# A two-layer attention / mLSTM step on one core: projection ahead of compression, page numbers read in eights, every order table written anew

## The chip, the cores and the metric

The kernel runs on one core of one Trainium2 chip. That core has a matrix engine (PE, with its weight loads shown apart as PEld), a vector engine (DVE), an activation engine (ACT), a general engine (POOL) and a sync engine (SP), whose queue issues most of the DMAs; ACT issues the rest. The metric is the device time of one execution in microseconds (us). Three runs of the kernel before took 1090.14, 1091.55 and 1093.12 us; their median is 1091.55 us.

## What is computed

One inference step of two layers, for a prompt of 512 tokens and 8 sample sequences with one new token each (520 token columns in all, width 1024). Layer 0 is sparse attention with three branches, layer 1 an mLSTM; a final norm follows. Cut to what this case touches:

```python
def nsa_project(h, w_in):                   # h = rmsnorm(x); one input projection
    p = h @ w_in                            # q | 6 k/v blocks of 256 columns | gates | z
    ...
def compress_branch(rows, pe, w1, b1, w2):  # rows: past pages and new tokens, two of the k/v blocks
    part = jnp.einsum('bnrchd,cjrde->bnjche', seg, w1r)     # segments of 16 rows, blocks of 32
    hid = ... + part[:, j:j + n_cmp, j]
    summ = jnp.einsum('bnche,ced->bnchd', jax.nn.silu(hid), w2)
def nsa_sample(h, cache_kv_l, cache_win_l, page_table, ...):
    past = cache_kv_l[page_table]           # 8 sequences x 8 pages of 128 rows
    ...                                     # attention over compressed, selected and window rows
# layer 1: mLSTM cell with its convolution, gates and matrix states; then rmsnorm
```

The results are the two outputs y, the new cache rows and the new states.

## The kernel before, in words

**Tiling.** Tokens lie along the free axis, 520 columns as two halves of 260 (`c` = 0 and 1); features lie on the 128 partitions. A product of float32 accuracy is three matmuls (`mm3`): weights and activations are each split into a high part (a rounded copy, `whi`, `hhi`, `phi`, `w1h`, made by ACT or by a copy on DVE, which the profile calls CAST) and a low part (the rest, `wlo`, `hlo`, `plo`, `w1l`, made by a subtraction on DVE or POOL); high times high, high times low and low times high are added in PSUM. `load_w` (L554) does this for one weight tile: a DMA to `wraw` (two buffers), `whi`, `wlo`.

**Stages.** There are seven lists of work, run one after the other: (1) norm of x, the 12 k/v projection tiles and the 16 compression units, with the gates (to about 224 us of the span, where PE ends its last transposes before the q projection); (2) the q and z projections (to about 330 us); (3) the attention units (to about 508 us); (4) the output projection and the mLSTM's input projection (to 673 us); (5) its z projection and gates (to 786 us); (6) the mLSTM cell (to about 1042 us); (7) the last of the output projection and the final norm.

**What sets the order.** In lists 1, 2, 4 and 7 every operation is recorded as a numbered piece, and a table of numbers (`CALLS0` to `CALLS3`) gives the order in which the pieces are issued. In lists 3, 5 and 6 operations carry names of what they read and write (class `Plan`), and the tables `ORDER0` to `ORDER2` give the order. Each engine then takes its own instructions strictly in that order, and waits with semaphores for the others. Tables `MOVED0` to `MOVED3` and `MOVEDP0` to `MOVEDP2` name pieces whose engine is exchanged (`swapped`): a high part from ACT to DVE or back, a subtraction, product or sum from DVE to POOL or back. Everything is issued through the recording layer, so nearly every instruction has line 498 in the profile, and tiles are told apart by name.

**List 1 in detail.** x comes in as `x_t`, four DMAs of half a column half each, into two of the three `praw` buffers; the first weight tile comes in two halves (`raw0`). `split_x` makes `hhi` and `hlo` of x; squares (`sq`) summed through a matmul with ones give the norm factor `rr`, which multiplies the projection only when PSUM is evacuated (`kvt<-mm,rr`). `kv_tile` (L843) is one projection tile: for each of the two column halves 24 matmuls (8 slices of three passes) in a PSUM bank of the kind `mm`, of which there are two. `cmp_unit` (L763) is one compression unit: eight pages of 128 KB from the cache (`pages`, L755) into one `praw` buffer, their high and low parts, and 48 matmuls against `w1`. A page's DMA takes its address from the page table in SBUF: SP reads one number into a register, checks it, and issues the DMA. `KB` is a tile of 128x4096 that POOL fills with zeros; `hlo_113` and `hhi_107` of the rows below are column half 0, `hlo_137` and `hhi_119` half 1 (in the changed program 192, 179 and 240, 219).

Of the kernel before, what the change touches and what calls it, by code (L numbers as in the profile page):

```python
# [17 lines left out]
T, NB, NTOK = 512, 8, 520  # L18
# [96 lines left out]
)  # L115
ORDER1 = (
# [418 lines left out]
def step_kernel(ctx, tc, ap):  # L535
# [22 lines left out]
    def mmb():  # L558
        return bank("mm", 2)
# [2251 lines left out]
```

## Time and profile before

| | |
|---|---|
| median of three runs | 1091.55 us |
| the profiled execution | 1091.77 us, of it 1089.9 us span |
| mean granted PE clock | 0.986 |
| PE busy | 1044.1 us (96%), 8567 instructions |
| DVE, ACT, POOL busy | 792.9, 578.4, 276.6 us |
| DMA | 197.18 MB, mean 181 GB/s |

Busy time by list, from the windows of the same execution:

| list | us of the span | PE | DVE | ACT | POOL | DMA share |
|---|---|---|---|---|---|---|
| 1 | 0 to 224 | 203.43 | 140.97 | 86.89 | 58.22 | 0.46 |
| 2 | 224 to 330 | 103.67 | 65.49 | 43.20 | 34.78 | 0.35 |
| 3 | 330 to 508 | 173.05 | 156.13 | 128.54 | 14.38 | 0.46 |
| 4 | 508 to 673 | 164.04 | 124.99 | 76.52 | 54.61 | 0.48 |
| 5 | 673 to 786 | 111.57 | 73.83 | 74.87 | 28.25 | 0.74 |
| 6 | 786 to 1042 | 252.98 | 198.14 | 152.73 | 75.47 | 0.80 |
| 7 | 1042 to 1090 | 35.34 | 33.40 | 15.62 | 10.93 | 0.34 |

"Busy" counts an engine as busy while any of its instructions is under way. Matmuls overlap, so a busy PE can still run below its pace; the count of matmuls in a stretch of fixed length tells that, and PEclk the clock that was granted. The chain of waits is followed back from the last instruction: at each step to what released it. A DMA queue of SP is shown as SPq; its instructions are not counted as busy time.

### The profile page before, as it was taken

How to read it: one execution, taken by the hardware profiler on the slowest of the kernel's cores; microseconds unless marked ns; L12 is line 12 of the kernel's file. 1: busy time of each engine (PE TensorE's matmuls, PEld its weight loads, DVE VectorE, ACT ScalarE, POOL GpSimd, SP SyncE). 2: the span in 40 equal slices, each digit the busy share in tenths (PEclk: the TensorE clock that was granted, in tenths of full speed). 3: DMA queues.
4: the chain of work that ended last, by engine and by line, in shares of the span. 5: the costliest groups of instructions: out<-in, count | busy, mean ns of one | idle time of the engine just before them, and what ended most of it. 6: DMA issues, size and time to landing. Idle time of an engine off the chain costs nothing.

```text
span 1089.9 us, 23970 instructions
## 1 busy us (share of the span) xinstructions
PE 1044.1 (96%) x8567; PEld 927.1 (85%) x8567; DVE 792.9 (73%) x1981; ACT 578.4 (53%) x1324; POOL 276.6 (25%) x301
## 2 busy tenths in 40 slices
PE   5999999999999999999999999999999999999996
PEld 4999899989998787778999999799867588887885
DVE  6856663578539899885788786757576778677886
ACT  5233243433358687773444455667666665654533
POOL 2215142222240100101234322231221333222322
PEclk9999999999999999999999999999999999999998
DMA  6454543233334642365543552878787789888542
GB/s 212 149 171 154 163 149 112 83 111 100 125 93 126 186 118 69 118 206 200 177 139 106 172 181 61 290 246 303 253 302 281 246 289 318 281 285 276 173 132 83
DMA packets 124793, 197.18 MB, mean 181 GB/s; under 512 B 16117, under 2 KB 66166, under 8 KB 124418
## 3 DMA queue, kind: packets, MB, share of 16 engines
q1 hardware_dynamic: 118194, 185.58, 52.4%
q10 hardware_dynamic: 6480, 10.08, 2.6%
q8 instruction: 67, 1.10, 0.4%
q14 instruction: 52, 0.43, 0.1%
HBM read 145.89 MB, written 58.10 MB: 187 GB/s over the span
## 4 chain that ended last, share of the span: by engine, by line
PE 75%; DVE 11%; ACT 5%; issue 3%; DMA 3%; SPq 2%; POOL 0%; POOLq 0%; DVEq 0%; ACTq 0%
PE mm L498 48%; PE s L498 15%; PE t L498 7%; PE d L498 5%; ACT s L498 2%; DVE s L498 2%; SPq L498 2%; DVE wlo L498 1%; DVE x L498 1%; DMA praw<-in_cache 1%; DMA wraw<-in_m_out 1%; DVE qst L498 1%; DVE sm L498 1%; ACT pt L498 1%; DMA wraw<-in_w_kv 1%
## 5 line engine op out<-in xcount | busy, mean ns | idle before, releaser
L498 PE MATMUL mm<-hhi,whi 128*128 128x260 f32 x976 | 282.4, 289 | 4.6 <-DVE kvt L498 3.2
L498 PE MATMUL mm<-hlo,whi 128*128 128x260 f32 x976 | 277.9, 285 | 4.1 <-DVE hlo L498 4.1
L498 PE MATMUL mm<-hhi,wlo 128*128 128x260 f32 x976 | 278.5, 285 | 2.0 <-DVE wlo L498 1.6
L498 PEld LDWEIGHTS mm<-hhi,whi 128*128 128x128 f32 x976 | 184.9, 189 | 10.1 <-DVE kvt L498 3.7
L498 PEld LDWEIGHTS mm<-hlo,whi 128*128 128x128 f32 x976 | 184.6, 189 | 5.0 <-DVE hlo L498 4.5
L498 PEld LDWEIGHTS mm<-hhi,wlo 128*128 128x128 f32 x976 | 184.8, 189 | 2.9 <-DVE wlo L498 2.3
L498 POOL TENSOR_TENSOR wlo<-wraw,whi 128x1024 fp32r<-128x1024 f32 (+1 forms) x50 | 104.0, 2080 | 257.9 <-ACT whi L498 192.8
L498 ACT ACTIVATE whi<-wraw 128x1024 fp32r<-128x1024 f32 (+1 forms) x79 | 69.8, 886 | 81.0 <-PE mm L498 61.9
L498 DVE SCALAR_TENSOR_TENSOR cs<-t,wk,cs 128x512 f32<-128x512 f32 x128 | 89.4, 743 | 17.8 <-ACT cs L498 8.3
L498 PE MATMUL s<-phi,w1h 128*128 128x256 f32 (+1 forms) x256 | 77.4, 302 | 2.1 <-ACT phi L498 2.1
L498 ACT ACTIVATE s<-s,mn 128x384 f32<-128x384 f32 (+3 forms) x128 | 70.7, 555 | 15.9 <-DVE mn L498 15.7
L498 ACT ACTIVATE cs<-cs,SBC 128x1024 f32<-128x1024 f32 x64 | 71.2, 1141 | 10.8 <-PE d L498 10.4
L498 PE MATMUL s<-plo,w1h 128*128 128x256 f32 (+1 forms) x256 | 74.9, 292 | 0.1
L498 PE MATMUL s<-phi,w1l 128*128 128x256 f32 (+1 forms) x256 | 74.5, 291 | 0.0
L498 PE MATMUL mm<-uh,whi 128*128 128x260 f32 x224 | 66.4, 296 | 3.0 <-DVE x L498 2.1
L498 PE MATMUL mm<-uh,wlo 128*128 128x260 f32 x224 | 64.3, 287 | 0.2 <-POOL wlo L498 0.2
L498 PE MATMUL mm<-ul,whi 128*128 128x260 f32 x224 | 64.0, 286 | 0.0
L498 DVE CUSTOM_DVE_ANT_0 s<-s,D 128x384 f32<-128x384 f32 (+3 forms) x128 | 59.7, 485 | 5.1 <-PE s L498 3.1
L498 DVE TENSOR_TENSOR wlo<-wraw,whi 128x1024 fp32r<-128x1024 f32 (+2 forms) x52 | 54.7, 1055 | 6.8 <-ACT whi L498 6.2
L498 PEld LDWEIGHTS s<-phi,w1h 128*128 128x128 f32 x256 | 48.9, 191 | 2.9 <-ACT phi L498 2.5
L498 PEld LDWEIGHTS s<-plo,w1h 128*128 128x128 f32 x256 | 48.7, 190 | 1.5 <-DVE plo L498 0.5
L498 PEld LDWEIGHTS mm<-uh,whi 128*128 128x128 f32 x224 | 43.0, 192 | 7.2 <-issue 2.2
(430 smaller groups left out, 2588.5 us busy)
## 6 DMA issues: line engine op xcount, KB each, us to landing
cs<-in_state_C SPq DMA_DIRECT2D x64, 512.0 KB, 5.8
o_cs<-cs SPq DMA_DIRECT2D x64, 512.0 KB, 4.3
praw<-in_cache SPq DMA_DIRECT2D x128, 128.0 KB, 2.3
dk<-in_cache SPq DMA_DIRECT2D x128, 128.0 KB, 2.3
wraw<-in_m_in SPq DMA_DIRECT2D x32, 512.0 KB, 3.6
wraw<-in_m_out SPq DMA_DIRECT2D x32, 256.0 KB, 4.1
wraw<-in_w_kv SPq DMA_DIRECT2D x11, 512.0 KB, 4.3
wraw<-in_w_q SPq DMA_DIRECT2D x8, 512.0 KB, 3.3
```

The lines of the kernel that those rows point to most:

```text
L498: return f(*[real(x) for x in a], **{n: real(x) for n, x in k.items()})
```

## The change

Four things change. (a) The six DMAs for x and the first weight tile are given to fixed queues: both halves of the first weight tile and x's second column half to SP, x's first column half to ACT. (b) The page numbers of a unit are read eight at a time by one load into eight registers, and the eight DMAs follow. (c) Three of the first six PSUM banks of the k/v projection are of another kind (`d` or `t` in place of `mm`), so that five of the first six column halves can be computed before the first is evacuated. (d) All order and exchange tables are new; the three of the plans, which were empty, now hold 50, 30 and 101 numbers.

```diff
-    for k, q in ((0, S), (1, SP)):
+    for k in range(2):
         ks = slice(4 * k, 4 * k + 4)
-        q.dma_start(raw0[:, ks], ap["w_kv"][0][:, ks])
+        SP.dma_start(raw0[:, ks], ap["w_kv"][0][:, ks])
         S.dma_start(xc[0][:, ks], ap["xT"][:, ks, 0:CH])
-    for k, q in ((0, S), (1, SP)):
+    for k in range(2):
         ks = slice(4 * k, 4 * k + 4)
-        q.dma_start(xc[1][:, ks], ap["xT"][:, ks, CH:NTOK])
+        SP.dma_start(xc[1][:, ks], ap["xT"][:, ks, CH:NTOK])
...
+        vs = []
         for i in range(8):
             def one(i=i):
-                v = SP.value_load(pt[0:1, row, u * 8 + i:u * 8 + i + 1], min_val=0, max_val=79)
-                SP.dma_start(dst(i), ap["cache"][bass.ds(v, 1), :, col:col + n].rearrange("o p f -> (o p) f"))
+                if not vs:
+                    vs.extend(nc.values_load_multi_w_load_instructions(
+                        real(pt[0:1, row, u * 8:u * 8 + 8]), engines=[mybir.EngineType.SP], min_val=0, max_val=79)[1])
+                SP.dma_start(dst(i), ap["cache"][bass.ds(vs[i], 1), :, col:col + n].rearrange("o p f -> (o p) f"))
...
-            po = mmb()
+            po = {(0, 1): db, (1, 1): xb, (2, 0): xb}.get((i, c), mmb)()
...
-MOVEDP0 = ()
...
+MOVEDP0 = (75, 78, 84, 113, 114, 193, 199, 229, 235, 308, 311, 314, 343, 429, 458, 459, 538, 544, 574, 653, 659, 689,
...
```

The tables themselves say nothing to a reader; what they do to the instructions is shown at three places.

**SP at the start of the program.** Before, the DMA queue begins so (`pt` is the page table, `nw` the norm weights, `TENSOR_LOAD` the reading of page numbers, `ISA` register instructions):

```order
L498 DMA pt<-in_page_table 1x128
L498 DMA nw<-in_norms 128x24
L498 TENSOR_LOAD pt
L498 ISA x3
L498 DMA praw<-in_cache 128x256
L498 DMA wraw<-in_w_kv 128x512
L498 DMA x_t<-in_xT 128x4x260
L498 DMA wraw<-in_w_kv 128x1024
L498 TENSOR_LOAD pt
```

Now:

```order
L506 DMA pt<-in_page_table 1x128
L506 DMA nw<-in_norms 128x24
L506 DMA pe<-in_pe 128x32
L506 DMA wraw<-in_w_kv 128x512 x2
L506 DMA x_t<-in_xT 128x4x260 x2
L769 TENSOR_LOAD pt
L769 ISA x16
L506 ISA
L506 DMA praw<-in_cache 128x256
```

The first weight tile and x's second half now stand ahead of every page, and one load with 16 register instructions stands ahead of eight pages where a load with three stood ahead of each. In the whole program the loads fall from 256 to 32.

**DVE around the first compression weights.** Before (`rv` and `rs_t` belong to the norm factor `rr`):

```order
L498 TENSOR_TENSOR wlo<-wraw,whi 128x1024
L498 TENSOR_TENSOR sq<-sq 128x260
L498 SCALAR_TENSOR_TENSOR hlo_137<-x_t,nw,hhi_119 128x260
L498 TENSOR_SCALAR rv<-s 128x260
L498 CAST w1h<-wraw 128x1024
L498 SCALAR_TENSOR_TENSOR hlo_137<-x_t,nw,hhi_119 128x260 x2
L498 TENSOR_TENSOR rs_t<-rs_y 128x260
L498 TENSOR_TENSOR w1l<-wraw,w1h 128x1024
L498 SCALAR_TENSOR_TENSOR rs_t<-rs_t,rv 128x260
L498 CAST phi<-praw 128x1024
```

Now, at the same place:

```order
L506 SCALAR_TENSOR_TENSOR hlo_240<-x_t,nw,hhi_219 128x260 x7
L506 TENSOR_TENSOR sq<-x_t 128x260 x2
L506 TENSOR_TENSOR sq<-sq 128x260
L506 TENSOR_TENSOR wlo<-wraw,whi 128x1024
L506 TENSOR_TENSOR plo<-praw,phi 128x1024
L506 TENSOR_TENSOR wlo<-wraw,whi 128x1024
L506 TENSOR_TENSOR sq<-x_t 128x260
L506 TENSOR_TENSOR sq<-sq 128x260
L506 TENSOR_SCALAR rv<-s 128x260
L506 TENSOR_TENSOR plo<-praw,phi 128x1024
```

All low parts of x now come ahead of the first `w1h`, and the low parts of two more weight tiles as well. On PE, accordingly, 63 projection matmuls stood ahead of the first compression matmul, and 120 do now (24 in `mm`, 24 in `d`, 48 in `t`, 24 in `mm`).

**POOL in the same stretch.** Before:

```order
L498 TENSOR_TENSOR sq<-x_t 128x260
L498 MEMSET KQ 128x256
L498 TENSOR_TENSOR sq<-sq 128x260
L498 MEMSET KB 128x4096
L498 TENSOR_TENSOR plo<-praw,phi 128x1024
```

Now:

```order
L506 MEMSET KQ 128x256
L506 ISA
L506 TENSOR_TENSOR rs_t<-rs_y 128x260
L506 MEMSET VC 128x1024
L506 TENSOR_TENSOR sq<-sq 128x260 x2
L506 TENSOR_TENSOR rs_t<-rs_y 128x260
L506 MEMSET KB 128x4096
```

The fill of `KB` moves behind the norm factor of the second column half (the second `rs_t`).

Counted over the whole program, PE keeps all its 7298 instructions. ACT has 1187 in place of 1232 and POOL 346 in place of 306. In list 3 DVE has 18 small copies (128x128 and 128x8x16) and three subtractions of 128x512 fewer, and six copies of 128x512 more; POOL has those three subtractions and two products of 128x256 more. In list 6 DVE takes 30 copies of 128x512 from ACT and gives eight subtractions of that size to POOL.

More of the change, by code (lines that the diff above doesn't have):

```diff
@@ L64 @@
 ORDER0 = (
[50 rows of a table removed]
[50 rows of a table added]
 )
 ORDER1 = (
[16 rows of a table removed]
[16 rows of a table added]
 )
 ORDER2 = (
[44 rows of a table removed]
[44 rows of a table added]
 )
 CALLS0 = (
[41 rows of a table removed]
[41 rows of a table added]
 )
 CALLS2 = (
[16 rows of a table removed]
[16 rows of a table added]
 )
 CALLS3 = (
[6 rows of a table removed]
-)
-MOVED0 = (
[6 rows of a table removed]
-)
-CALLS1 = (
[33 rows of a table removed]
-)
-MOVED1 = (
[5 rows of a table removed]
-)
-MOVED2 = (4, 8, 9, 27, 65, 66, 84, 122, 142, 160, 161, 177, 185, 198, 210, 212, 213, 225, 227, 243, 249, 274, 280,
-    283, 289, 320, 326, 333, 347,)
-MOVED3 = (2, 12, 27, 30, 35, 37, 44, 52, 65, 69, 85, 90, 94, 99, 103, 120, 124,)
-MOVEDP0 = ()
-MOVEDP1 = ()
-MOVEDP2 = ()
[6 rows of a table added]
+)
+MOVED0 = (13, 15, 29, 37, 45, 53, 58, 66, 67, 71, 74, 75, 82, 83, 87, 96, 100, 101, 112, 140, 160, 164, 169, 179,
[8 rows of a table added]
+CALLS1 = (
[33 rows of a table added]
+)
+MOVED1 = (27, 29, 30, 43, 45, 52, 69, 71, 72, 73, 88, 89, 104, 105, 112, 117, 126, 127, 133, 138, 157, 167, 169, 184,
[6 rows of a table added]
+MOVED2 = (4, 8, 9, 27, 66, 104, 122, 123, 141, 142, 161, 175, 176, 178, 182, 197, 198, 204, 213, 219, 225, 228, 240,
+    242, 249, 267, 274, 280, 282, 289, 295, 307, 308, 320, 333, 347,)
+MOVED3 = (2, 12, 20, 22, 27, 30, 37, 44, 51, 52, 69, 85, 90, 94, 99, 103, 120, 124,)
+MOVEDP0 = (75, 78, 84, 113, 114, 193, 199, 229, 235, 308, 311, 314, 343, 429, 458, 459, 538, 544, 574, 653, 659, 689,
+    695, 716, 765, 774, 803, 846, 878, 907, 910, 943, 952, 956, 965, 970, 980, 990, 995, 1005, 1015, 1019, 1021,
+    1037, 1040, 1044, 1045, 1047, 1050, 1053,)
+MOVEDP1 = (16, 32, 37, 46, 52, 72, 76, 87, 97, 102, 106, 107, 112, 127, 132, 136, 137, 142, 147, 151, 157, 166, 167,
+    192, 197, 202, 212, 225, 230, 335,)
+MOVEDP2 = (3, 75, 177, 272, 285, 287, 288, 289, 307, 309, 319, 328, 331, 333, 339, 346, 356, 369, 389, 391, 393, 399,
[4 rows of a table added]
 KSC = float(np.float32(512.0 ** -0.5))
```

441 rows, old and new, of tables (CALLS0, CALLS1, CALLS2, CALLS3) are left out of this document.

## The prediction

> **What bounds the kernel now.** I read the page first, then windows of 5 us, then the chain of waits, then the timeline where the windows show holes.
>
> ```profile
> span 1089.9 us, 23970 instructions
> PE 1044.1 (96%) x8567; PEld 927.1 (85%) x8567; DVE 792.9 (73%) x1981; ACT 578.4 (53%) x1324; POOL 276.6 (25%) x301
> PE 75%; DVE 11%; ACT 5%; issue 3%; DMA 3%; SPq 2%; POOL 0%; POOLq 0%; DVEq 0%; ACTq 0%
> ```
>
> PE is the bound, and its instructions are the same after the change; so only its holes can be won, and its slow stretches. Where they lie, list 1 shows by the count of matmuls in 5 us (first bracket), the granted clock (third number from the end) and the DMA rate (last):
>
> ```profile
> 15.00:20.00 5.00, 3.79 (x17) 3.20 (x15) 4.42 (x10) 3.41 (x9) 0.38 (x1) 1.00 0.59 186
> 20.00:25.00 5.00, 1.71 (x13) 1.51 (x13) 5.00 (x4) 1.05 (x5) 3.92 (x2) 0.96 0.33 104
> 25.00:30.00 5.00, 4.48 (x24) 4.24 (x25) 4.72 (x8) 1.06 (x1) 2.24 (x1) 0.69 0.51 157
> 45.00:50.00 5.00, 5.00 (x44) 5.00 (x43) 4.72 (x9) 1.40 (x5) 2.44 (x2) 1.00 0.68 214
> 65.00:70.00 5.00, 3.54 (x17) 2.84 (x16) 2.00 (x4) 3.48 (x9) 0.87 (x1) 0.90 0.30 88
> 70.00:75.00 5.00, 5.00 (x26) 4.82 (x26) 2.96 (x7) 1.38 (x6) 0.00 (x0) 0.76 0.58 182
> 120.00:125.00 5.00, 2.33 (x15) 2.32 (x15) 4.68 (x7) 0.00 (x0) 0.00 (x0) 0.86 0.46 159
> 125.00:130.00 5.00, 5.00 (x35) 4.95 (x35) 3.92 (x11) 1.74 (x9) 0.10 (x1) 0.80 0.47 157
> 200.00:205.00 5.00, 3.98 (x23) 3.94 (x24) 2.70 (x9) 1.46 (x6) 0.84 (x1) 1.00 0.34 125
> ```
>
> Full pace is about 43 in 5 us (x44 counts both edges). Three holes stand out: up to 30, 65 to 75, 120 to 130; and in each the clock drops after PE has waited, so that the stretch behind a wait is slow too. The chain in order of time (start, length) says what PE waited for:
>
> ```profile
> 4.67 6.16 DMA wraw<-in_w_kv
> 17.91 1.23 DVE wlo L498
> 20.21 4.26 DVE w1h L498
> 61.63 4.87 DMA praw<-in_cache
> 74.05 5.79 PE mm L498 x48
> 115.34 4.79 issue
> 188.95 2.20 DMA praw<-in_cache
> ```
>
> The first hole is the first weight tile's DMA and then DVE; the second is pages (`praw`), and so is the third by the wait of DVE shown next. Why pages are late is seen in SP's queue, beside a DVE instruction that waited:
>
> ```profile
> 105.25 12.09 SPq L498 DMA_DIRECT2D praw<-in_cache  x9
> 160.42 36.71 SPq L498 DMA_DIRECT2D praw<-in_cache  x30
> praw<-in_cache SPq DMA_DIRECT2D x128, 128.0 KB, 2.3
> L498 SPq DMA_DIRECT2D praw<-in_cache x16: 332/333/612, 171.1 to 188.9; - x16
> 120.22 0.69 DVE L498 CAST phi<-praw 128x1024 fp32r<-128x1024 f32 x1 [4.88 <-issue]
> ```
>
> SP issues 30 pages in 36.71 us, 1.22 us each, of which the DMA instruction is 0.33 us: the rest is the reading of the page number. A page lands 2.3 us after its issue, so the data is not late; the issue is. The DMA engines moved only 88 to 218 GB/s in these windows.
>
> **The change part by part.** The sum is made against the profiled execution, 1091.77 us: its span of 1089.9 and 1.87 around it, 0.2 above the median of 1091.55.
>
> *Head (parts a, c and the new order).* Before, the stretch around the hole runs so:
>
> ```profile
> 11.51 0.69 DVE L498 TENSOR_TENSOR wlo<-wraw,whi 128x512 fp32r<-128x512 f32 x1 [0.56 <-ACT whi L498]
> 19.05 0.42 DVE L498 TENSOR_TENSOR sq<-sq 128x260 f32<-128x260 f32 x1
> 19.39 0.48 DVE L498 SCALAR_TENSOR_TENSOR hlo<-x_t,nw,hhi 128x260 fp32r<-128x260 f32 x1
> 20.13 4.34 DVE L498 CAST w1h<-wraw 128x1024 fp32r<-128x1024 f32 x1
> 20.42 3.51 POOL L498 MEMSET KB<- 128x4096 f32 x1
> 24.92 0.59 PE L498 MATMUL mm<-hlo,whi 128*128 128x260 f32 x1 [3.29 <-DVE hlo L498]
> 27.00 0.68 DVE L498 CAST phi<-praw 128x1024 fp32r<-128x1024 f32 x1
> 31.92 1.41 PE s L498 x12
> ```
>
> The copy `w1h` took 4.34 us where a copy of that size takes 0.68: it stood against POOL's fill of `KB`, with x's low parts queued behind it and PE behind those. Compression began at 31.92, with 63 projection matmuls done. Now the first weights no longer queue behind pages and the rest of x, so DVE can work on from about 5 us (4.67 in the chain), without the wait to 10.83. DVE's queue up to the first `w1l` holds 16 low parts of x at 0.48 (7.7 us), two half and two whole `wlo` (1.4 and 2.5), two half copies (0.7), two `plo` of that size (2.5), ten squares or sums (4.2), five operations of the norm factor and the first bias product (2.0), `w1h` (0.7) and `w1l` (1.2): 22.9 us, so about 27.6 at the earliest. Compression then starts up to 4.3 us earlier, and with 120 projection matmuls done in place of 63: 57 times 0.121 (5.79 us for 48) is 6.9 us of PE work that no longer lies behind. Both together are 11 us, if DVE never waits. As the other end I take that only the hole before 24.92 goes, 3.3 us. I take 7, nearer the sum of what PE lost between its first projection matmul and 30 us: by the windows from 20 to 30, 43+43-13-24 = 49 matmuls, 5.9 us, and a little from the earlier weights. The evacuations are later, but five banks hold what is not evacuated; that is the cover, and if `d` or `t` is wanted sooner, one tile's 24 matmuls (2.9 us) wait.
>
> *Page numbers in eights (b).* A batch is one load and some 17 register instructions, then eight DMAs at 0.33. No row shows such a load. At worst each page still costs 1.22; at best the 0.89 us beside the DMA is paid once in eight, 0.33 + 0.11, or 3.5 us for a unit of eight in place of 9.8. Nearest is the single read, so I take about 0.7 a page. A unit and a projection tile keep PE busy for 2 x 5.79 = 11.6 us; SP then has 5.6 us of pages in that time, and is no longer late. The holes are worth, in matmuls short of 43: 26+17 at 65 to 75 (5.2 us), 28+8 at 120 to 130 (4.4 us). What is late next is a free `praw` buffer and the splitting on DVE (140.97 of 224 us busy). I take 7 of the 9.6, ends 0 and 9.6. Behind 188.95 the windows are short too, but the work there is also a chain of small transposes: I take 1.5 of the 20 matmuls missing at 200 to 205 (2.4 us), ends 0 and 3.
>
> The skill says the opposite of what the queue shows. The Trainium skill, page "DMA: Bandwidth & Descriptors", section "Issuing engines are not separate DMA queues", calls the time to initiate a DMA "usually small relative to the DMA itself"; by that the reading of numbers would hide behind the transfers, this part would be worth nothing, and the sum would be 8.5 us higher. The 36.71 us for 30 pages speak against it here.
>
> *KB's fill (d).* It now runs behind the second `rs_t`, at some 35 us, and still takes 3.5 us. A copy `phi` of DVE may again stand against it; PE then has a run of 84 compression matmuls queued, of which half need it not. I take 1 us of loss, ends 0 and 5 (3.5 and a slow-clock stretch like the 1.5 us lost at 25 to 30). The Trainium skill, page "SBUF — State Buffer", section "Who interferes with whom", says that a DVE instruction with two SBUF inputs contends with a GpSimd instruction that reads SBUF, not with one that only writes. By that only copies stand against a fill, the `plo` beside it run on, and the loss would be at most one copy's wait; the 4.34 us copy agrees.
>
> *Lists 2 to 7 (orders and exchanges).* They hold few holes; the largest is in list 3, where DVE is nearly full:
>
> ```profile
> 360.00:380.00 20.00, 17.80 (x231) 15.16 (x231) 17.53 (x62) 13.98 (x40) 4.82 (x2) 0.91 0.78 219
> 365.33 3.50 DVE L498 TENSOR_SCALAR s<-s,sm 128x384 f32<-128x384 f32 x4
> 366.20 2.42 POOL L498 TENSOR_TENSOR wlo<-wraw,whi 128x1024 fp32r<-128x1024 f32 x1 [8.27 <-ACT whi L498]
> 369.24 0.80 PE L498 MATMUL s<-cst,s 128*128 128x128 f32 x3 [1.51 <-DVE mn L498]
> L498 DVE COPY dpt<-t 128x128 f32<-128x128 f32 x13 | 3.7, 284 | 0.1
> L498 DVE TENSOR_TENSOR uo<-u,uo 128x512 fp32r<-128x512 f32 x7 | 4.8, 684 | 0.3 <-ACT uo L498 0.3
> L498 POOL TENSOR_TENSOR ul<-num,uh 128x512 fp32r<-128x512 f32 x7 | 9.7, 1386 | 3.4 <-ACT uh L498 2.3 <-issue 1.1
> ```
>
> DVE gives away 18 copies at 0.28 and three subtractions at 0.68 (7.1 us) and takes six 128x512 copies, 0.6 each by the subtraction (about 4): 3 us less of 156.13. Against that, each POOL subtraction lasts 1.39 us, in which DVE can be held. In list 6 PE is busy for 252.98 of 256 us, so DVE's extra 30 copies have cover, as long as DVE (198.14) stays below it. I take 0, ends -5 and +6: a hole as at 366 (1.5 us and about as much of slow clock) either twice gone or twice added.
>
> Sum: -7 - 7 - 1.5 + 1 + 0 = -14.5, so 1077.3 by the profiled execution and 1077 by the median.
>
> **The rivals.** *Slower: POOL holds DVE in list 3.* One event as at 366 costs PE 1.51 us and, by the clock of 0.91 over 20 us, 1.8 more: 3.3. POOL gets three subtractions and two products more there, and other moments for its `wlo`. From five more events on (16 us) the head's gain is gone; with six or seven (21 us) the time is 1098. For it: DVE busy 156 of 178 us. Against it: DVE's own load falls.
>
> *Pages stay late*, because the batch's reads take as long, or the buffers bind: without the 8.5 us, 1085. For it: no row shows the batch. Against it: a DMA rate far below the 352 GB/s that the window from 5 to 10 us reaches:
>
> ```profile
> 5.00:10.00 5.00, 4.30 (x8) 2.18 (x8) 2.98 (x8) 3.64 (x10) 0.00 (x0) 1.00 1.05 352
> ```
>
> *Given back*: the small transposes that end list 1 (23 matmuls at 200 to 205) wait for something that comes at its old time, or list 1's gain meets new holes: 1091. Against it: the chain there names pages.
>
> *More than that*: the full 11 and 9.6, 3 at 200, and 5 in the later lists: 1063 to 1068, 1066.
>
> **How the numbers follow.** The forecast 0.55 (own range 1071 to 1083), pages late 0.13, more 0.10, given back 0.09, slower 0.13. About 0.3%, 3.3 us, is what a measurement can tell from no change. Faster by more is the first three, 0.78; the same 0.09; slower 0.13. The range that leaves out 0.2 reaches from the upper case on one side to the given-back case on the other: 1066 to 1091.
>
> **What would show it.** Right: compression's first matmul at 27 to 30 us behind 120 projection matmuls; page issues about 0.7 us apart; over 40 matmuls in every 5 us from 45 to 180; list 1 ending near 210. Wrong: DVE waiting for `praw` with SP's pages 1.2 us apart; a copy of several microseconds beside `KB`'s fill with PE idle; list 3 lasting over 185 us, or more half-clock stretches than seven.

## The result, and the profile after

Four runs of the changed kernel took 1071.78 to 1073.29 us, median 1073.02, against 1092.1 for the kernel before (four runs, 1090.14 to 1093.12). The ratio is 0.9825, 95% interval 0.9808 to 0.9842: 19.1 us faster, where 14.5 was forecast. The profiled execution took 1072.83 us, 18.9 less than the one before. The page gives its span and busy times:

```profile
span 1071.1 us, 23676 instructions
PE 1036.5 (97%) x8567; PEld 921.8 (86%) x8567; DVE 798.7 (75%) x1984; ACT 548.1 (51%) x1281; POOL 304.6 (28%) x341
```

The span is 18.8 us shorter. PE's busy time fell by 7.6 us (from 1044.1) with the same 8567 matmuls; the other 11.2 is time in which PE stood still. The 7.6 fits the granted clock: a mean of 0.986 over 1089.9 us is a loss of 15.3 us, and 0.993 over 1071.1 us one of 7.5. This is an estimate, since the clock is also low in stretches where PE stands.

The windows of list 1 that answer to the holes of before (busy time and count of PE, PEld, DVE, ACT, POOL; granted clock; DMA share; GB/s):

```profile
15.00:20.00 5.00, 5.00 (x39) 4.82 (x38) 4.63 (x10) 4.61 (x10) 0.00 (x0) 1.00 0.44 148
20.00:25.00 5.00, 5.00 (x44) 5.00 (x43) 4.96 (x8) 2.79 (x6) 0.92 (x2) 1.00 0.89 257
25.00:30.00 5.00, 5.00 (x44) 5.00 (x44) 4.90 (x7) 1.79 (x3) 1.79 (x3) 1.00 0.53 169
45.00:50.00 5.00, 4.00 (x34) 3.79 (x33) 3.36 (x8) 3.79 (x7) 0.00 (x0) 1.00 0.77 243
65.00:70.00 5.00, 5.00 (x38) 4.97 (x37) 4.39 (x14) 2.54 (x8) 0.76 (x1) 1.00 0.96 300
120.00:125.00 5.00, 5.00 (x44) 4.95 (x43) 4.57 (x9) 2.30 (x5) 0.10 (x1) 1.00 0.47 150
200.00:205.00 5.00, 3.58 (x26) 2.71 (x25) 3.33 (x12) 3.37 (x12) 0.25 (x1) 1.00 0.00 0
205.00:210.00 5.00, 4.58 (x25) 4.10 (x25) 1.83 (x2) 2.51 (x7) 3.09 (x3) 0.66 0.11 36
```

From 15 to 30 us PE now runs 127 matmuls in place of 54; the holes at 65 and 120 are gone (38 at 65 with PE busy throughout are the longer matmuls of 384 columns), and a hole of 1 us is left at 45 to 50. The small transposes that end list 1 wait as before, and a slow stretch follows them (a clock of 0.66 from 205 us).

Three tile groups give the landmarks used below: duration of one (min/median/max, ns), then first and last start in us. They are the first high-times-high matmul of compression, the page DMAs, and the first matmul of list 3.

```profile
L506 PE MATMUL s<-phi,w1h x256: 275/282/531, 28.6 to 201.3; 128*128 128x256 f32 x112, 128*128 128x384 f32 x16
L506 SPq DMA_DIRECT2D praw<-in_cache x128: 332/333/892, 8.5 to 175.8; - x128
L506 PE MATMUL s<-KA,qst x128: 222/367/507, 309.9 to 470.3; 128*128 128x256 f32 x32, 128*128 128x512 f32 x32, 128*128 128x128 f32 x32, 128*128 128x384 f32 x32
```

The same groups of the kernel before:

```profile
L498 PE MATMUL s<-phi,w1h x256: 275/282/882, 31.8 to 217.7; 128*128 128x256 f32 x112, 128*128 128x384 f32 x16
L498 SPq DMA_DIRECT2D praw<-in_cache x128: 332/333/670, 3.1 to 196.8; - x128
L498 PE MATMUL s<-KA,qst x128: 220/386/628, 327.8 to 491.6; 128*128 128x256 f32 x32, 128*128 128x512 f32 x32, 128*128 128x128 f32 x32, 128*128 128x384 f32 x32
```

Compression starts 3.2 us earlier, behind 57 more projection matmuls; the last page is issued 21.0 us earlier; list 3 starts 17.9 us earlier. So 17.9 of the 18.8 us are won by the end of list 2, and lists 3 to 7 together add 0.9.

### The profile page after: what moved, and what is told of

Read it like the earlier page. It is cut to its first block, busy times and chain, and to the rows that moved or that the text cites. A ratio compares the mean times of both kernels' runs of the same rounds, so it can differ in the third digit from the quotient of the medians.

```text
span 1071.1 us, 23676 instructions
## 1 busy us (share of the span) xinstructions
PE 1036.5 (97%) x8567; PEld 921.8 (86%) x8567; DVE 798.7 (75%) x1984; ACT 548.1 (51%) x1281; POOL 304.6 (28%) x341
## 5 line engine op out<-in xcount | busy, mean ns | idle before, releaser
L506 PE MATMUL mm<-hhi,whi 128*128 128x260 f32 (+1 forms) x952 | 274.3, 288 | 1.1 <-DVE kvt L506 0.4
L506 PE MATMUL mm<-hhi,wlo 128*128 128x260 f32 (+1 forms) x952 | 270.7, 284 | 1.0 <-DVE wlo L506 0.6
L506 PE MATMUL mm<-hlo,whi 128*128 128x260 f32 (+1 forms) x952 | 270.0, 284 | 0.5 <-DVE hlo L506 0.5
L506 PEld LDWEIGHTS mm<-hhi,whi 128*128 128x128 f32 (+1 forms) x952 | 179.3, 188 | 6.4 <-issue 3.9
L506 PEld LDWEIGHTS mm<-hhi,wlo 128*128 128x128 f32 (+1 forms) x952 | 179.1, 188 | 1.8 <-DVE wlo L506 1.0
L506 PEld LDWEIGHTS mm<-hlo,whi 128*128 128x128 f32 (+1 forms) x952 | 178.9, 188 | 1.3 <-DVE hlo L506 0.8
L506 DVE SCALAR_TENSOR_TENSOR cs<-t,wk,cs 128x512 f32<-128x512 f32 x128 | 89.2, 744 | 11.2 <-ACT cs L506 6.4
L506 ACT ACTIVATE s<-s,mn 128x256 f32<-128x256 f32 (+3 forms) x128 | 70.8, 555 | 12.3 <-DVE mn L506 11.7
L506 ACT ACTIVATE whi<-wraw 128x1024 fp32r<-128x1024 f32 (+1 forms) x52 | 45.8, 881 | 49.6 <-PE mm L506 20.9
L506 DVE CUSTOM_DVE_ANT_0 s<-s,D 128x256 f32<-128x256 f32 (+3 forms) x128 | 59.4, 487 | 5.5 <-PE s L506 4.5
```

The source lines that it names most:

```text
L506: return f(*[real(x) for x in a], **{n: real(x) for n, x in k.items()})
```

## The experiments

The landmarks below come from the same groups of each kernel's profile, in us:

| kernel | compression starts | last page issued | last compression matmul | list 3 starts | profiled time |
|---|---|---|---|---|---|
| before | 31.8 | 196.8 | 217.7 | 327.8 | 1091.77 |
| changed | 28.6 | 175.8 | 201.3 | 309.9 | 1072.83 |
| before, reads in eights | 31.2 | 179.4 | 207.7 | 317.4 | 1079.07 |
| changed, single reads | 28.0 | 204.0 | 224.5 | 332.9 | 1095.04 |
| changed, reads in pairs | 28.7 | 196.7 | 219.5 | 328.8 | 1093.52 |
| before, eights, fill late | 27.2 | 175.7 | 204.0 | 313.9 | 1076.32 |
| changed, fill early | 30.0 | 179.3 | 204.9 | 313.9 | 1074.96 |

The first column varies with one and the same list 1: the kernel before with only lists 2 to 7 new starts compression at 34.5 us and list 3 at 327.7. The start of list 3 is the steadier landmark: with the changed list 1 it lies at 309.0 to 310.1 us in six profiles.

### The reads alone, and everything but the reads

The kernel before, with only the reads in eights:

```diff
+        vs = []
         for i in range(8):
             def one(i=i):
-                v = SP.value_load(pt[0:1, row, u * 8 + i:u * 8 + i + 1], min_val=0, max_val=79)
-                SP.dma_start(dst(i), ap["cache"][bass.ds(v, 1), :, col:col + n].rearrange("o p f -> (o p) f"))
+                if not vs:
+                    vs.extend(nc.values_load_multi_w_load_instructions(
+                        real(pt[0:1, row, u * 8:u * 8 + 8]), engines=[mybir.EngineType.SP], min_val=0, max_val=79)[1])
+                SP.dma_start(dst(i), ap["cache"][bass.ds(vs[i], 1), :, col:col + n].rearrange("o p f -> (o p) f"))
```

> The kernel before, with only the page numbers read eight at a time; queues, banks and all order tables as before. Theory (the prediction's part b): SP's pages fall from 1.22 us to about 0.5 us each (after the change 8 pages took 3.97 us), the page holes at 65 to 75 and 120 to 130 close, and the time is 1092 - 7 = 1085 us (ends 1082 and 1089); list 1 ends 6 to 9 us earlier, and the head up to 31.9 us is unchanged. Rival 'order': the holes were closed by the place of the pages in SP's order; then the reads alone change the time by less than 2 us (1090 to 1094).

Measured: 1080.22 us (1074.87 to 1081.59) against 1089.71, ratio 0.99, interval 0.9867 to 0.9933: 9.5 us less, where the theory had 7 (3 to 10). Its copy `w1h` still stands against the fill, and list 3 starts 10.4 us earlier than before:

```profile
18.43 4.34 DVE L498 CAST w1h<-wraw 128x1024 fp32r<-128x1024 f32 x1
```

```profile
L498 SPq DMA_DIRECT2D praw<-in_cache x128: 332/333/1180, 5.1 to 179.4; - x128
L498 PE MATMUL s<-KA,qst x128: 220/384/654, 317.4 to 481.3; 128*128 128x256 f32 x32, 128*128 128x512 f32 x32, 128*128 128x128 f32 x32, 128*128 128x384 f32 x32
```

The two later holes are gone with the old order (PE alone: busy time and count, clock, DMA share, GB/s); 31 matmuls with PE busy throughout are again those of 384 columns:

```profile
65.00:70.00 5.00, 5.00 (x31) 1.00 0.57 191
120.00:125.00 5.00, 5.00 (x41) 1.00 0.88 280
```

So the reads are worth 9.5 us by themselves, and the rival that the order closed the holes falls. Then the reverse edit, in the changed kernel:

```diff
-        vs = []
         for i in range(8):
             def one(i=i):
-                if not vs:
...
-                SP.dma_start(dst(i), ap["cache"][bass.ds(vs[i], 1), :, col:col + n].rearrange("o p f -> (o p) f"))
+                v = SP.value_load(pt[0:1, row, u * 8 + i:u * 8 + i + 1], min_val=0, max_val=79)
+                SP.dma_start(dst(i), ap["cache"][bass.ds(v, 1), :, col:col + n].rearrange("o p f -> (o p) f"))
```

> The changed kernel, with the page numbers read one by one again; everything else as changed. Theory: the page holes return, since the order now asks for pages earlier behind 120 projection matmuls; 1073 + 7 = 1080 us (ends 1077 and 1084), with SP's pages 1.2 us apart and DVE waiting for praw. Rival 'order': the time stays within 2 us of 1073.

Measured: 1094.78 us (1090.49 to 1098.27), ratio to before 1.0043, interval 1.0021 to 1.0065. The theory (1077 to 1084) had the direction, and the time lies more than 10 us above its upper end. All the rest of the change, without the reads, is a loss of some 5 us; the reads are worth 22 us there, more than twice what they are worth in the old order. The windows show what comes back:

```profile
115.00:120.00 5.00, 2.69 (x16) 2.34 (x15) 0.06 (x1) 1.42 (x3) 4.54 (x2) 0.87 0.63 219
145.00:150.00 5.00, 0.79 (x3) 0.49 (x3) 3.48 (x7) 1.63 (x3) 2.94 (x1) 0.94 0.03 10
150.00:155.00 5.00, 4.74 (x22) 4.74 (x23) 2.25 (x6) 2.13 (x6) 3.52 (x3) 0.50 0.42 137
185.00:190.00 5.00, 1.74 (x14) 1.53 (x14) 3.05 (x4) 1.94 (x4) 0.00 (x0) 1.00 0.34 111
```

```profile
L506 SPq DMA_DIRECT2D praw<-in_cache x128: 332/333/850, 6.2 to 204.0; - x128
```

The holes are as deep as before the change, with a whole stretch at a clock of 0.50 behind one. The table says why: where pages are read singly, the last compression matmul comes 20.9 us (before) and 20.5 us (changed, single) after the last page is issued; with eights the distance is 25 to 28 us. So with single reads the end of list 1 follows SP's page queue. PE's waits from 28 to 232 us sum to 18.9 us there, 8.9 in the kernel before and 4.5 in the changed one. Compression starts at 28.0 us, 3.8 earlier than before, and the time is still longer: by this reading the early start only brings PE to the wait for pages sooner. Why the last page is 7 us later than before (204.0 against 196.8) is settled in part: 3 us of it are there at the first page (6.2 against 3.1), and between 60 and 204 us SP's queue waits some 39 us for tiles to come free, some 24 in the kernel before. Which moves of the new order lengthen these waits was not tried.

### Reads in pairs

```diff
-        vs = []
+        vs = {}
...
-                if not vs:
-                    vs.extend(nc.values_load_multi_w_load_instructions(
-                        real(pt[0:1, row, u * 8:u * 8 + 8]), engines=[mybir.EngineType.SP], min_val=0, max_val=79)[1])
+                if i // 2 not in vs:
+                    o = u * 8 + i // 2 * 2
+                    vs[i // 2] = nc.values_load_multi_w_load_instructions(
+                        real(pt[0:1, row, o:o + 2]), engines=[mybir.EngineType.SP], min_val=0, max_val=79)[1]
```

> The changed kernel, with page numbers read two at a time. By the runs before, a page costs SP 1.22 us read singly and 0.50 us in eights (3.97 us for 8); 0.33 of it is the DMA instruction, so a read is 0.82 us for the load and 0.07 us for each number, and in pairs a page costs 0.33 + 0.41 + 0.07 = 0.81 us, a unit of eight 6.5 us. Theory 'supply against demand': 9 projection tiles remain beside the 16 units after the first three, so PE works 5.8 + 9/16 x 5.8 = 9.1 us for a unit; 9.8 us (singly) is too slow, 6.5 us is enough, and the time is within 3 us of the changed kernel: 1073 to 1076 us. Rival 'every microsecond of page reading counts': the loss goes with the cost of a page, (0.81 - 0.50)/(1.22 - 0.50) of 22 us, 9.5 us: 1082 us.

Measured: 1091.58 us (1088.44 to 1095.14), ratio 1.0018, interval 0.9998 to 1.0038. The theory of supply against demand falls by 15 us; the rival, at 1082, missed by almost 10, since the price of a pair was wrong too. SP's rows show the price of a read: the first pages follow a DMA of x with nothing but the read between. In the changed kernel (eight numbers), with pairs, and with single reads, and for each a run of eight pages later on:

```profile
5.00 0.38 SPq L506 DMA_DIRECT2D x_t<-in_xT  x1
8.50 1.42 SPq L506 DMA_DIRECT2D praw<-in_cache  x3
...
26.60 3.97 SPq L506 DMA_DIRECT2D praw<-in_cache  x8
```

```profile
4.53 0.38 SPq L506 DMA_DIRECT2D x_t<-in_xT  x1
6.46 2.50 SPq L506 DMA_DIRECT2D praw<-in_cache  x3
...
28.01 7.15 SPq L506 DMA_DIRECT2D praw<-in_cache  x8
```

```profile
4.70 0.38 SPq L506 DMA_DIRECT2D x_t<-in_xT  x1
6.16 2.67 SPq L506 DMA_DIRECT2D praw<-in_cache  x3
...
25.73 8.16 SPq L506 DMA_DIRECT2D praw<-in_cache  x8
```

Reading one number takes 1.08 us (6.16 - 5.08), two 1.55, eight 3.12: some 0.3 us for each number, which a batch does not save, and 0.8 once. Between two pages later on a single read is cheaper: eight pages of 0.33 with seven reads between take 8.16 us, 0.79 for a read, and 0.19 is left from page to page where no read stands between (3.97 us). A unit of eight costs SP 3.12 + 3.97 = 7.1 us in eights, 0.89 a page; about 1.55 + 7.15 = 8.7 in pairs; 1.08 + 8.16 = 9.2 singly. By these prices, a loss in proportion is (8.7 - 7.1)/(9.2 - 7.1) of 21.8 us, 16.6 us, or 1089.6 us; 1091.58 was measured. The rival, that every microsecond of page reading counts, comes within 2 us once its price is put right from this run's own rows; no further run tried it. The other theory went by a mean over 16 units. That pages are asked for in bursts and wait for one of three buffers, so that SP cannot work ahead in the quiet stretches, would explain the miss. SP's rows agree: in the changed kernel 29 pages from 140.87 us on take 35.28 us, and for 11.8 of them the queue waits for earlier pages to be split, so that their tile comes free. With other numbers of buffers this was not tried.

### The head: the fill of KB and the queues

In the kernel before with reads in eights, the number of the fill (3) moves in list 1's table to behind the second half's norm factor (98):

```diff
-    100, 56, 184, 3, 57, 185,
+    100, 56, 184, 57, 185,
...
+    98, 3,
```

> The kernel before with page numbers read in eights (1080 us), and POOL's fill of KB moved behind the norm factor of the second column half; nothing else. Theory (the prediction's head: the 4.34 us copy stood against the fill, with x's low parts and PE behind it): the copy w1h falls to about 0.7 us, the hole of PE before 25 us closes, and 3.3 us go: 1077 us (ends 1075 and 1078.5), compression's first matmul at 27.5 to 29 in place of 31.2. Rival 'something else comes as late': DVE waits for the next page or weight, or the fill holds another copy at its new place; 1079.5 us or more.

Measured: 1077.79 us (1074.93 to 1079.44), ratio 0.9888, interval 0.9867 to 0.991; by medians 2.4 us less than with the reads alone, of two chips, which their intervals cannot tell apart. The profile shows the step plainly: the copy falls from 4.34 to 0.89 us, compression starts at 27.2 in place of 31.2, and list 3 starts 3.5 us earlier.

```profile
17.68 0.89 DVE L496 CAST w1h<-wraw 128x1024 fp32r<-128x1024 f32 x1
...
27.77 3.64 DVE L496 TENSOR_SCALAR acc<-wraw,pe 128x128 f32<-128x128 f32 x1
27.96 3.45 DVE L496 SCALAR_TENSOR_TENSOR hlo<-x_t,nw,hhi 128x260 fp32r<-128x260 f32 x1
```

```profile
27.80 3.53 POOL L496 MEMSET KB<- 128x4096 f32 x1
```

At its new place the fill meets another instruction: a `TENSOR_SCALAR` of DVE lasts until the fill ends (0.77 us in the changed kernel), and so does the `hlo` behind it. The fill came to a cheaper place here, not to a free one.

The reverse in the changed kernel, the fill put back behind `w1h` (100):

```diff
+    100, 3,
...
-    303, 3, 315,
+    303, 315,
```

> The changed kernel, with POOL's fill of KB moved back to stand right behind the copy w1h of DVE in the order, as before the change. Theory: the copy (1.11 us there) takes 4 us or more, w1l and compression's first matmul come some 3 us later (31 to 32 in place of 28.6), and PE has no projection left to cover it: 1073 + 3 to 5 = 1077 us (ends 1075 and 1079). Rival 'covered': 120 matmuls ahead hide it; within 1.5 us of 1073.

Measured: 1074.61 us (1073.98 to 1077.37), ratio 0.9862, interval 0.9842 to 0.9882: 1.6 us more than the changed kernel, between the theory's lower end (1075) and the rival's bound (1074.5). Compression starts at 30.0, earlier than the 31 to 32 of the theory. DVE and POOL there:

```profile
25.06 4.22 DVE L504 TENSOR_SCALAR acc<-wraw,pe 128x128 f32<-128x128 f32 x1
25.26 4.55 DVE L504 CAST w1h<-wraw 128x1024 fp32r<-128x1024 f32 x1
```

```profile
25.68 3.51 POOL L504 MEMSET KB<- 128x4096 f32 x1
```

Both DVE instructions last until the fill ends, 3.4 us more than in the changed kernel, whose `w1h` and fill stand apart:

```profile
25.45 1.11 DVE L506 CAST w1h<-wraw 128x1024 fp32r<-128x1024 f32 x1
...
39.12 1.22 DVE L506 TENSOR_TENSOR plo<-praw,phi 128x1024 fp32r<-128x1024 f32 x1
...
41.33 0.69 DVE L506 CAST phi<-praw 128x1024 fp32r<-128x1024 f32 x1 [0.34 <-DMA praw<-in_cache]
...
42.59 1.22 DVE L506 TENSOR_TENSOR plo<-praw,phi 128x1024 fp32r<-128x1024 f32 x1
```

```profile
36.88 3.52 POOL L506 MEMSET KB<- 128x4096 f32 x1
```

Beside the later fill the subtraction at 39.12 takes the same 1.22 us as the one at 42.59, away from it, and the next copy, which waits for a page, starts after the fill. That agrees with the Trainium skill, page "SBUF — State Buffer", section "Who interferes with whom": copies, casts and `tensor_scalar` can take the pair of ports that DVE shares with GpSimd, and an instruction with two SBUF inputs contends with a GpSimd instruction that reads SBUF, not with one that only writes. In the profile list 3 starts 4.0 us later with the early fill (313.9 against 309.9), and some 2 us of that are gone again by the end (1074.96 against 1072.83).

Last of the head, the queues of x and the first weights as before, in the changed kernel:

```diff
-    for k in range(2):
+    for k, q in ((0, S), (1, SP)):
         ks = slice(4 * k, 4 * k + 4)
-        SP.dma_start(raw0[:, ks], ap["w_kv"][0][:, ks])
+        q.dma_start(raw0[:, ks], ap["w_kv"][0][:, ks])
...
-        SP.dma_start(xc[1][:, ks], ap["xT"][:, ks, CH:NTOK])
+        q.dma_start(xc[1][:, ks], ap["xT"][:, ks, CH:NTOK])
```

> The changed kernel, with the six DMAs of x and the first weight tile on the queues of before (one half of each on ACT, one on SP, by the same order table). Theory: DVE's 23 us of work set the start of compression, not the first weights; the first projection matmul may come 1 to 3 us later, compression starts at most 1 us later: 1073 to 1074.5 us. Rival 'the first weights set the head': the first weight half lands as late as before the change (10.8 in place of 7.3) and the time is 1076 us or more.

Measured: 1073.31 us (1072.56 to 1079.99), ratio 0.9859, interval 0.9833 to 0.9885; its profiled execution has the changed kernel's span, 1071.1 us. The first projection matmul starts at 7.4 us there and at 7.9 in the changed kernel. Before the change it starts at 15.5, and at 13.8 with the reads alone in eights. Part (a) is worth nothing that can be told; what brought the first matmul forward is then the order, the one part left that touches it. Part (c), the three other banks, was not tried by itself.

### Lists 2 to 7

The tables of lists 2 to 7 as before, in the changed kernel (`CALLS2`, `ORDER0`, `CALLS1`, `ORDER1`, `ORDER2`, `CALLS3` and their exchange tables, of which one is shown), and then the reverse, these new tables alone in the kernel before:

```diff
-MOVEDP0 = (75, 78, 84, 113, 114, 193, 199, 229, 235, 308, 311, 314, 343, 429, 458, 459, 538, 544, 574, 653, 659, 689,
...
+MOVEDP0 = ()
```

> The changed kernel, with the order and exchange tables of lists 2 to 7 as before; queues, banks, page reads and list 1's tables as changed. Theory 'all of it is list 1': the lead at the end of list 1 (16.7 us after the change) is kept to the end, so 1092 - 17 = 1075 us (ends 1073 and 1077); the new tables of lists 2 to 7 are worth 2 us at most. Rival 'the later lists paid': without their new tables part of the lead is lost in lists 2 to 7 again, and the time is 1080 us or more. Rival 'the later lists cost': 1070 us or less.

```diff
-MOVEDP0 = ()
+MOVEDP0 = (75, 78, 84, 113, 114, 193, 199, 229, 235, 308, 311, 314, 343, 429, 458, 459, 538, 544, 574, 653, 659, 689,
...
```

> The kernel before, with only the order and exchange tables of lists 2 to 7 as changed. Theory 'all of it is list 1': 1090 us (ends 1087 and 1093), list 3 about 3.6 us shorter, lists 6 and 7 together 1 to 3 us longer. Rival 'the later lists paid': 1085 us or less. Rival 'POOL holds DVE in list 3' (from the prediction): 1095 us or more.

Measured: with list 1 alone new, 1071.28 us (1069.9 to 1073.54), ratio 0.9826, interval 0.9793 to 0.9859, the ratio of the whole change. By its microseconds that lies between the theory's lower end (1073) and the bound of 'the later lists cost' (1070); the ratio, taken against the kernel before on the same chip, speaks for the theory, without shutting that rival out. With lists 2 to 7 alone new, 1088.85 us (1086.18 to 1092.48), ratio 0.9987, interval 0.9969 to 1.0006. So the whole gain is list 1's, with its queues, banks and reads. But the zero of the later lists is a sum. List 3 and list 6, each from its own first matmul to that of the next list, in the kernel before (its windows; columns as above):

```profile
327.80:501.70 173.90, 169.15 (x1966) 137.42 (x1962) 155.57 (x629) 129.57 (x413) 14.88 (x24) 0.99 0.46 138
788.00:1052.70 264.70, 261.28 (x1587) 202.00 (x1586) 206.11 (x439) 155.76 (x264) 78.80 (x90) 0.99 0.79 265
```

and in the changed kernel:

```profile
309.90:480.20 170.30, 167.36 (x1965) 136.59 (x1963) 151.62 (x613) 131.02 (x424) 21.82 (x35) 1.00 0.44 129
767.90:1035.80 267.90, 263.16 (x1585) 202.41 (x1585) 222.38 (x478) 134.72 (x224) 92.10 (x97) 0.99 0.76 260
```

List 3 wins 3.6 us, list 6 loses 3.2. With the old tables, list 3 takes 173.7 to 174.2 us in four profiles and list 6 263.1 to 264.7 in five; with the new ones list 3 takes 170.1 to 170.7 in nine and list 6 267.5 to 269.7 in seven. So list 6 was given its old tables:

```diff
-ORDER2 = (
-    316, 290, 291, 593, 303, 294, 292, 306, 342, 21, 341, 1, 22, 92, 5, 31, 0, 13, 307, 295, 2, 522, 282, 293,
+ORDER2 = (
+    291, 290, 292, 593, 294, 303, 306, 286, 341, 288, 21, 32, 1, 408, 22, 295, 342, 5, 0, 13, 307, 293, 2, 10,
...
-MOVEDP2 = (3, 75, 177, 272, 285, 287, 288, 289, 307, 309, 319, 328, 331, 333, 339, 346, 356, 369, 389, 391, 393, 399,
...
+MOVEDP2 = ()
```

> The changed kernel, with the order and exchange tables of list 6 (the mLSTM cell) as before. In the runs so far lists 2 and 3 took 272 to 274 us with the new tables and 277 with the old, and lists 6 and 7 took 294 to 295 with the new and 290 to 292 with the old. Theory 'list 6 gives back what list 3 won': lists 6 and 7 fall to 291 us, and the time is 1070 us (ends 1068.5 and 1071.5), below both kernels. Rival 'noise of single profiles': 1072 us or more.

Measured: 1068.64 us (1068.2 to 1072.76), ratio 0.9819, interval 0.9795 to 0.9843. List 6 falls back to 264.7 us, and the profiled execution, 1068.59 us, is 4.2 below the changed kernel's. Its median is the lowest here, as forecast (1068.5 to 1071.5); its ratio lies below that of the two kernels with the full new tables timed beside it (0.9859 and 0.9862), but its interval covers the changed kernel's 0.9825.

Which of order and exchange makes the loss, and which the gain in list 3, three kernels tell: the changed kernel without list 3's exchanges (`MOVEDP0 = ()`), without list 6's (`MOVEDP2 = ()`), and with list 6's old `ORDER2` under its new exchanges.

```diff
-MOVEDP0 = (75, 78, 84, 113, 114, 193, 199, 229, 235, 308, 311, 314, 343, 429, 458, 459, 538, 544, 574, 653, 659, 689,
...
+MOVEDP0 = ()
```

> The changed kernel with list 3 (the attention units) in the new order, but without its 50 exchanges of engines. List 3 took 173.9 to 174.2 us with the old tables and 170.2 to 170.3 with the new. Theory 'less work on DVE': the exchanges made the gain (DVE busy 151.6 us in place of 155.5), and list 3 goes back to 173 to 175 us, the time to 1076 or 1077 us. Rival 'order': list 3 stays at 170 to 171 us and the time at 1073. Rival of the prediction 'POOL holds DVE': without the exchanges list 3 gets shorter than 170 us.

```diff
-MOVEDP2 = (3, 75, 177, 272, 285, 287, 288, 289, 307, 309, 319, 328, 331, 333, 339, 346, 356, 369, 389, 391, 393, 399,
...
+MOVEDP2 = ()
```

> The changed kernel with list 6 (the mLSTM cell) in the new order, but without its 101 exchanges of engines. List 6 took 264.7 us with the old tables (1068.6 us in all) and 267.9 with the new (1073 us). Theory 'too much on DVE': the exchanges, which raise DVE's busy time there from 206 to 222 us, made the loss, and list 6 takes 265 us, the time 1069 to 1070 us. Rival 'order': list 6 stays at 267 us or more, and the time at 1072 us or more.

```diff
-ORDER2 = (
-    316, 290, 291, 593, 303, 294, 292, 306, 342, 21, 341, 1, 22, 92, 5, 31, 0, 13, 307, 295, 2, 522, 282, 293,
...
+ORDER2 = (
+    291, 290, 292, 593, 294, 303, 306, 286, 341, 288, 21, 32, 1, 408, 22, 295, 342, 5, 0, 13, 307, 293, 2, 10,
```

> The changed kernel with list 6 in the order of before, but with the 101 new exchanges of engines. List 6 took 264.7 us with both tables old, 267.9 with both new, 272.0 with the new order alone; that refuted the theory that the exchanges make the loss. Theory 'the new order costs and its exchanges win part of it back': with the old order the exchanges at least do no harm, list 6 takes 262 to 265 us, the time is 1066 to 1069 us. Rival 'the tables only fit each other': the exchanges in the old order put work on DVE where it is not free (30 copies more), list 6 takes 268 us or more, the time is 1073 us or more.

Measured, in this order: 1084.83 us (ratio 0.9953, interval 0.9935 to 0.9972), 1076.85 (0.9873, 0.9847 to 0.99) and 1081.73 (0.9931, 0.9909 to 0.9953). The windows of the list concerned, one for each kernel:

```profile
309.70:492.20 182.50, 172.47 (x1965) 138.86 (x1963) 159.37 (x631) 130.97 (x414) 16.13 (x25) 0.98 0.39 121
```

```profile
767.80:1039.80 272.00, 262.69 (x1587) 202.78 (x1587) 208.73 (x445) 154.88 (x264) 76.97 (x90) 0.99 0.75 256
```

```profile
766.70:1045.10 278.40, 265.16 (x1585) 203.19 (x1585) 229.56 (x477) 135.00 (x224) 92.19 (x97) 0.98 0.73 251
```

| list 6 | old exchanges (none) | new exchanges (101) |
|---|---|---|
| old order | 264.7 | 278.4 |
| new order | 272.0 | 267.9 |

None of the three theories held. The exchanges do not make list 6's loss: without them the new order takes 4.1 us more, in the old order they cost 13.7. In list 3 the theory had the direction alone: the new order without its exchanges takes 182.5 us where 173 to 175 were expected, 12.2 more than with them and 8.6 more than before. In list 6, where all four pairs ran, neither table is good or bad alone. DVE's busy time does not rank them: 208.7 us goes with 272.0 and 222.4 with 267.9. Which waits make the difference was not followed up.

## Why the prediction was right, and where it was not

The 1073.02 us lie inside both ranges, 4 us below the forecast. By its steps:

- **What bounds the kernel.** Right: PE's holes and slow stretches. PE stands still 11.2 us less; the 7.6 us less of busy time fit the clock.
- **Head, -7.** Right in size: with the reads in eights already there, the rest of the change brings list 3 from 317.4 to 309.9, 7.5 us, of which the fill's place alone gave 3.5 in one profile. Compression starts at 28.6 (27 to 30 forecast). That the first weights no longer stand behind pages is the work of the order; the other queues (part a) give nothing that can be told. What the step left out is its condition: with single reads the same rest, head and all, makes the kernel 5 us slower than before.
- **Page numbers in eights, -7.** Right mechanism, term too small: 10.4 us by list 3's start and 9.5 by medians, beside an upper end of 9.6. The price of a page was wrong in the other direction, 0.89 us in place of 0.7, since each number costs 0.3 us in the batch too. Nor was all of the 1.22 us before the reading of the number: of the 36.71 us for 30 pages the queue waited 2.7 for a page tile to come free. The holes of before were worth all of the term. The wait for a free buffer that was feared is there, but it took nothing of the term: the pages from 140.87 us on are 1.22 us apart as before, and PE has no hole there. "Pages stay late" (1085) falls with this. The Trainium skill, page "DMA: Bandwidth & Descriptors", section "Issuing engines are not separate DMA queues", speaks of the time to initiate a DMA, and for that the trace agrees: 0.33 us beside 2.3 us to landing. What the prediction read into it, that the reading of numbers hides too, is what fell: the 9.5 us and the 22 us are of the reads alone.
- **Region 185 to 210, -1.5.** Did not come: 26 and 25 matmuls in the last two windows, and a clock of 0.66. From the last compression matmul to the end of list 1 it is 6.1 us (201.3 to 207.4), and 6.4 before (217.7 to 224.1). What PE waited for from 28 to 210 us, in all, times, longest:

```profile
PE s L506 <- ACT phi L506: 1.0, 1, 1.0
PE t L506 <- DVE KQ L506: 0.9, 1, 0.9
PE s L506 <- DVE plo L506: 0.7, 3, 0.3
PE t L506 <- DVE VNEW L506: 0.5, 1, 0.5
...
PE t L506 <- ACT VC L506: 0.4, 1, 0.4
```

The transposes (`t`) wait for small copies of this chain (`KQ`, `VNEW`, `VC`), and the last page was issued 24 us before their window, so the end of list 1 waits for no page there.
- **KB's fill, +1.** Nothing: no copy stood against it at its new place. That "only copies stand against a fill" was too narrow: `TENSOR_SCALAR` does too, 3.64 us in the kernel before with eights and the fill late, 4.22 in the changed kernel with the fill early. In the changed kernel none stands beside the fill.
- **Lists 2 to 7, 0.** Right as a sum, for no reason given: list 3 won 3.6 us and list 6 lost 3.2. That DVE's additional copies "have cover" in list 6 was not what counted, as the four combinations show. "POOL holds DVE in list 3" falls: with POOL's new work the list got shorter.
- **The sum.** It added terms of list 1 as if each kept its worth beside the others. Put in first, the reads win 9.5 us and the rest loses 5; put in last, the reads win 22 and the rest 7 (1080.2 to 1073.0). The total came out near since the head's 7 is its worth once the reads are in, and the term of the reads is near their worth before the head is. That was luck: the prediction gives no order in which its terms are to be put in.
- **The signs.** The start of compression and the end of list 1 (207.4, "near 210") came as named. Over 40 matmuls in every 5 us did not (34 at 45 to 50, 29 at 70 to 75), nor did pages 0.7 us apart.

## What to carry to other kernels

When one queue feeds the bound engine, ask of every gain ahead of it whether the queue can follow: the rest of this change was worth 7.5 us with fast page reads and less than nothing without them. A batch saves only what is paid per batch, so read the price per item from the trace first. And an order table and the engines its operations run on belong together: against the old pair of list 6, the new order without its exchanges cost 7.3 us and the new exchanges in the old order 13.7, where the two full pairs differ by 3.2.

## What the runs showed of the hardware that was not expected

- Reading a number from SBUF into an SP register, with its check, costs 0.3 us each even eight at a time: 1.08, 1.55 and 3.12 us for one, two and eight numbers at the start of the program, beside 0.33 for the DMA instruction.
- 7.6 of the 18.8 us are busy time of PE and not idle time; the estimate from the granted clock (15.3 - 7.5 us) is as large. PE's busy time for the same 8567 matmuls goes with the holes: 1044.1 us before and again with single reads in the changed kernel, 1036.5 after, 1033.6 with list 6's old tables.
- A fill by POOL held a copy of DVE and a `TENSOR_SCALAR` until its end (4.55 and 4.22 us), and left a subtraction at its 1.22 us.
